# The last row block of a matmul with RMS norm: another split of the last product, squares shared between two engines, GpSimd for gamma, and the last stores reordered

## The chip, the cores and the metric

The kernel runs on one core of one Trainium2 chip. The core's engines work side by side: TensorE forms the matrix products, VectorE, ScalarE and GpSimd work element by element, SyncE issues transfers, and the DMA engines carry them out. A "store" is a transfer of finished output out of the core. The metric is device time of one execution in microseconds (us), as the median of several executions. Every ratio comes with a 95% interval. A "profile" is one execution recorded by the hardware profiler, which lists each instruction with its start, its length and what released it.

## The reference

```python
def reference(a, b, gamma, eps):          # a, b: 2048 x 2048 float32
    x = np.matmul(a, b)
    rms = np.sqrt(np.mean(x ** 2, axis=-1, keepdims=True) + eps)
    return (gamma * x / rms).astype(np.float32)
```

A row of the output can only be finished when its whole row of `x` is known, because `rms` needs the sum of all its squares.

## The kernel before

The product is cut into pairs of 128-row blocks, and each pair is formed with seven products in place of eight (sums and differences of quarter blocks). Columns are handled in four chunks of 512. The change touches only the end of the last pair: row block `rb`, whose four chunks can leave the core only after the very last product. That product completes chunk 3 (`x22[1]`). It is done in two halves, so that the first half is added and squared while TensorE works on the second.

The names in the excerpt are these. `p6` holds the result banks of the product. `t[1]` is what has to be added to it. `gam[c]` is gamma for chunk c. `xb` holds chunks 0 and 1, `x22[1]` chunk 3 and `p4[1]` chunk 2. `msq[rb]` holds the sums of squares of the chunks that are finished. `r_b` is the reciprocal of rms.

```python
        add(t[1], t[1], p4[1], ALU.subtract)            # VectorE
        square(rb, p4[1])                               # ScalarE: msq[rb][:, 2]
        pre_b = partial(rb)                             # VectorE: msq columns 0 and 1, and eps
        half_sq = stat_pool.tile([P, 2], FP32, name="n2")
        halves = [slice(0, CH // 2), slice(CH // 2, CH)]
        # [cut: TensorE, 8 matmuls for each half into p6]
        for h, col in enumerate(halves):
            add(x22[1][:, col], p6[h], t[1][:, col])    # VectorE
            sq = sq_pool.tile([P, 2 * CH], BF16, name="sq")   # a pool with ONE buffer
            nc.scalar.activation(out=sq[:, 0:CH // 2], in_=x22[1][:, col], func=ACTF.Square,
                                 scale=inv_sqrt_n, accum_out=half_sq[:, h:h + 1])
        part = stat_pool.tile([P, 1], FP32, name="part")
        nc.vector.tensor_scalar(out=part, in0=half_sq[:, 0:1], scalar1=pre_b,
                                scalar2=msq[rb][:, 2:3], op0=ALU.add, op1=ALU.add)
        add(x22[0], x22[0], gam[1], ALU.mult)           # VectorE: chunk 1 by gamma
        r_b = inverse_rms(half_sq[:, 1:2], part)        # ScalarE root, VectorE reciprocal
        x = xb[:, 0:CH]
        nc.vector.tensor_scalar_mul(out=x, in0=x, scalar1=r_b)
        nc.sync.dma_start(out=rows(rb, 0, CH), in_=x)   # store 1, SyncE's queue
        x = xb[:, CH:]
        by_r(x, r_b)                                    # ScalarE
        nc.scalar.dma_start(out=rows(rb, CH, HALF), in_=x)   # store 2, ScalarE's queue
        for c, x, src in ((3, x22[1], x22[1]), (2, x21[1], p4[1])):
            scaled_gamma(x, src, r_b, gam[c])           # VectorE: times r and gamma
            nc.sync.dma_start(out=rows(rb, c * CH, (c + 1) * CH), in_=x)   # stores 3, 4
```

The argument needs one thing that experiment 1 shows: where an instruction of an engine waits, those written behind it on that engine wait as well.

## Time and profile before

| What | Value |
|---|---|
| Time, median (range) of 3 runs | 224.39 us (224.30 to 224.49) |
| Span in the profile | 222.6 us |
| Share of the chain that ended last: TensorE | 83% |
| End of the last matmul (timeline) | 214.68 us |
| r usable | 216.35 us |
| Last four stores issued | 216.87, 217.11, 217.53, 218.19 us |
| Packets of these stores (DMA records) | 217.7 to 221.07 us |

This is the line of the profile page that gives the chain of work that ended last, by engine, for the kernel before. TensorE has 83% of it, and the change leaves TensorE's columns as they are, so only the tail after 214.68 us can move.

```profile
PE 83%; DMA 8%; DVE 2%; POOL 2%; issue 1%; ACT 1%; DVEq 0%; ACTq 0%; POOLq 0%
```

These lines are the timeline of the kernel before: start in us, length in us, engine (DVE is VectorE, ACT ScalarE, PE TensorE, SPq and ACTq the store queues of SyncE and ScalarE), source line, operation, output<-input, shapes, and in brackets the idle time ahead of it with what ended it.

```profile
214.02 0.60 ACT L291 ACTIVATE sq<-acc 128x512 bf16<-128x512 f32 x1 [0.67 <-DVE x L617]
214.03 0.42 DVE L617 TENSOR_TENSOR x<-acc,x 128x256 f32<-128x256 f32 x1
...
214.72 0.42 DVE L617 TENSOR_TENSOR x<-acc,x 128x256 f32<-128x256 f32 x1 [0.26 <-PE acc L677]
...
215.61 0.19 ACT L682 ACTIVATION_READ_ACCUMULATOR sq<-x 128x1 f32 x1
215.83 0.29 ACT L328 ACTIVATE rms<-n,part 128x1 f32<-128x1 f32 x1
216.16 0.16 DVE L322 RECIPROCAL r<-rms 128x1 f32<-128x1 f32 x1
...
216.35 0.48 DVE L690 TENSOR_SCALAR x<-x,r 128x512 f32<-128x512 f32 x1
...
216.87 0.33 SPq L691 DMA_DIRECT2D out_dram<-x  x1
217.11 0.36 ACTq L694 DMA_DIRECT2D out_dram<-x  x1
...
217.53 1.05 SPq L697 DMA_DIRECT2D out_dram<-x  x2
```

The first half is added at 214.03, before TensorE has finished. The second follows 0.04 us after the last matmul, at 214.72. ScalarE squares three things one after the other and has its last sum at 215.80. Then come root and reciprocal, and the first store leaves at 216.87. The last line merges two stores, 217.53 and 218.19.

The view by stretches of the kernel before has, for each us of the tail, the busy time of each engine with instruction counts, and in its last three columns the granted TensorE clock, the share of the DMA engines that is busy, and GB/s:

```profile
217.00:218.00 1.00, 0.00 (x0) 0.00 (x0) 1.00 (x2) 0.07 (x1) 0.00 (x0) 1.00 0.29 109
218.00:219.00 1.00, 0.00 (x0) 0.00 (x0) 0.16 (x1) 0.00 (x0) 0.00 (x0) 1.00 1.04 363
219.00:220.00 1.00, 0.00 (x0) 0.00 (x0) 0.00 (x0) 0.00 (x0) 0.00 (x0) 0.66 1.05 324
220.00:221.00 1.00, 0.00 (x0) 0.00 (x0) 0.00 (x0) 0.00 (x0) 0.00 (x0) 0.50 0.79 254
```

From 218 to 220 the DMA engines are full (the share can come out a little over 1), and after VectorE's last 0.16 us nothing else works: the 1.05 MB of the last row block are leaving the core.

### The profile page before, as it was taken

The page shows a single profiled execution, that of the slowest core. Times are in us where ns is not written, and L with a number is a line of the kernel's source. Part 1 is how long each engine was busy: PE and PEld are TensorE (multiplying, and loading weights), DVE is VectorE, ACT ScalarE, POOL GpSimd, SP SyncE. Part 2 cuts the span into 40 slices and gives each one's busy share as a digit, 9 for nine tenths or more (in the row PEclk, how much of TensorE's full clock was granted, in tenths as well). Part 3 has the DMA queues.
Part 4 walks back from the last instruction along what each step waited for, and adds up shares of the span by engine and source line. Part 5 has one row for each costly group of instructions (what it writes and reads, how often), then busy time and mean ns, then how long its engine had stood idle before and what let it go on. Part 6 is the DMA issues. An engine that isn't in the chain of part 4 may idle for free.

```text
span 222.6 us, 3026 instructions
## 1 busy us (share of the span) xinstructions
PE 211.1 (95%) x1043; PEld 98.6 (44%) x1043; DVE 161.8 (73%) x324; ACT 129.1 (58%) x272; POOL 24.5 (11%) x49
## 2 busy tenths in 40 slices
PE   7899999999999999999999999999999999999950
PEld 2445444444454444444444444444444444444430
DVE  2427557983999989978949298837994589587692
ACT  3110002807698895799646985699478954334570
POOL 7534232300000001000100002000200000000000
PEclk9999999999999999999999999999999999999997
DMA  6999999999973499818889259945994794044045
GB/s 184 223 202 209 203 208 211 212 303 259 327 280 159 188 272 292 310 72 226 276 228 400 58 174 222 366 151 143 246 368 168 97 282 189 0 188 193 0 190 188
DMA packets 36176, 47.13 MB, mean 212 GB/s; under 512 B 21952, under 2 KB 26048, under 8 KB 34496
## 3 DMA queue, kind: packets, MB, share of 16 engines
q0 software_dynamic: 9648, 23.33, 41.6%
q1 hardware_dynamic: 26080, 22.29, 33.0%
q10 hardware_dynamic: 432, 1.31, 2.0%
q8 instruction: 8, 0.13, 0.2%
q14 instruction: 8, 0.07, 0.1%
HBM read 34.60 MB, written 16.78 MB: 231 GB/s over the span
## 4 chain that ended last, share of the span: by engine, by line
PE 83%; DMA 8%; DVE 2%; POOL 2%; issue 1%; ACT 1%; DVEq 0%; ACTq 0%; POOLq 0%
PE acc L279 63%; PE acc L350 18%; DMA b<-in_b_dram 8%; POOL early L106 1%; DVE x L617 1%; POOL b L100 1%; DVE x L620 1%; PE tbank L179 1%; PE tbank L382 1%; PE tbank L165 1%; ACT sq L291 0%; DVEq L732 0%; ACT sq L682 0%; DVE x L690 0%; DVE r L322 0%
## 5 line engine op out<-in xcount | busy, mean ns | idle before, releaser
L279 PE MATMUL acc<-b,s 128*128 128x512 bf16 x376 | 83.3, 379 | 0.0
L279 PEld LDWEIGHTS <-s 128*128 128x128 f16 x472 | 46.2, 98 | 55.7 <-DVE s L244 0.2
L350 PE MATMUL acc<-b,head_at 128*128 128x512 bf16 x240 | 55.1, 379 | 0.6 <-DMA b<-in_b_dram 0.4
L291 ACT ACTIVATE sq<-x 128x512 bf16<-128x512 f32 x62 | 39.1, 631 | 10.9 <-DVE x L520 5.1
L340 DVE SCALAR_TENSOR_TENSOR x<-x,r,gamma_sb 128x1024 f32<-128x1024 f32 x28 | 34.7, 1282 | 0.8
L209 ACT ACTIVATE sq<-a 128x1024 bf16<-128x1024 f32 x24 | 25.4, 1057 | 16.8 <-DMA a<-in_a_dram 16.4
L350 PEld LDWEIGHTS <-head_at 128*128 128x128 bf16 x240 | 22.9, 98 | 26.7 <-issue 1.1
L393 ACT COPY x<-acc 128x512 f32<-128x512 f32 x11 | 5.9, 591 | 25.1 <-PE acc L350 25.1
L231 ACT ACTIVATE head_at<-a,s 128x2048 f16<-128x2048 f32 x10 | 19.9, 1990 | 0.0
L279 PEld LDWEIGHTS <-at_even 128*128 128x128 f16 x96 | 9.4, 98 | 11.5 <-issue 0.4
L279 PEld LDWEIGHTS <-head_at 128*128 128x128 f16 x96 | 9.4, 98 | 11.3
L100 POOL DMA_DIRECT2D b<-in_b_dram x15 | 10.6, 708 | 16.0 <-DMA b<-in_b_dram 13.2
L217 DVE TENSOR_SCALAR s<-norm 128x1 f32<-128x1 f32 x12 | 1.8, 150 | 14.3 <-ACT norm L212 14.2
L244 DVE TENSOR_TENSOR s<-at_even 128x1024 f16<-128x1024 f16 x15 | 9.7, 684 | 2.8 <-DMA at_even<-head_at 2.8
L291 ACT ACTIVATION_READ_ACCUMULATOR sq<-x 128x1 f32 x62 | 11.7, 188 | 0.0
L279 PE MATMUL acc<-t_left,s 128*128 128x512 bf16 x48 | 11.3, 379 | 0.0
L279 PE MATMUL acc<-early,s 128*128 128x512 bf16 x48 | 11.3, 379 | 0.0
L279 PE MATMUL acc<-early,at_even 128*128 128x512 bf16 x48 | 11.0, 379 | 0.0
L279 PE MATMUL acc<-t_left,at_even 128*128 128x512 bf16 x48 | 10.9, 379 | 0.0
L509 ACT COPY x<-acc 128x512 f32<-128x512 f32 x10 | 5.7, 575 | 8.9 <-PE acc L279 8.9
L279 PE MATMUL acc<-t_left,head_at 128*128 128x512 bf16 x48 | 10.8, 379 | 0.0
L279 PE MATMUL acc<-early,head_at 128*128 128x512 bf16 x48 | 10.8, 379 | 0.0
(86 smaller groups left out, 205.8 us busy)
## 6 DMA issues: line engine op xcount, KB each, us to landing
out_dram<-x SPq DMA_DIRECT2D x30, 512.0 KB, 3.1
a<-in_a_dram POOLq DMA_DIRECT2D x12, 1024.0 KB, 8.5
b<-in_b_dram POOLq DMA_DIRECT2D x15, 512.0 KB, 17.1
early<-in_a_dram POOLq DMA_DIRECT2D x7, 256.0 KB, 14.8
early<-in_b_dram ACTq DMA_DIRECT2D x2, 512.0 KB, 5.9
gamma_sb<-in_gamma_dram POOLq DMA_DIRECT2D x1, 1024.0 KB, 19.9
out_dram<-x SPq DMA_DIRECT2D x3, 256.0 KB, 3.5
early<-in_a_dram SPq DMA_DIRECT2D x1, 512.0 KB, 5.7
```

What stands on the lines that cost most here:

```text
L100: nc.gpsimd.dma_start(out=raw[j][kp], in_=b[kp * W2:(kp + 1) * W2, j * HALF:(j + 1) * HALF].rearrange("(t p) n -> p t n", p=P))
L106: nc.gpsimd.dma_start(out=ah(kp), in_=a[0:HB * P, kp * W2:(kp + 1) * W2].rearrange("(r p) k -> p r k", p=P))
L165: nc.tensor.matmul(view[:, t, r, :], ah(kp)[:, r, t * P:(t + 1) * P], identity, is_transpose=True, start=(t == 0 and r == 0), stop=(t == 1 ...
L209: nc.scalar.activation(out=junk, in_=a32[mb][:, h * HALF:(h + 1) * HALF], func=ACTF.Square, scale=2.0 ** -8, accum_out=n2[:, h:h + 1])
L231: nc.scalar.activation(out=a16[mb], in_=a32.pop(mb), func=ACTF.Copy, scale=factor.pop(mb))
L244: nc.vector.tensor_tensor(out=s_sum[s], in0=x, in1=y, op=op)
L279: nc.tensor.matmul(bank, lhsT[:, kp, :], rhs, start=(start and kp == 0), stop=(kp == KP - 1), skip_group_check=not start)
L291: nc.scalar.activation(out=sq[:, 0:CH], in_=src, func=ACTF.Square, scale=inv_sqrt_n, accum_out=msq[mb][:, c:c + 1])
L340: nc.vector.scalar_tensor_tensor(out=x, in0=x, scalar=r, in1=gamma_sb[:, h * HALF:(h + 1) * HALF], op0=ALU.mult, op1=ALU.mult)
L350: nc.tensor.matmul(bank, head_at[:, kt, r, :], head_rhs(c, kt), start=(kt == 0), stop=(kt == KT - 1))
L393: copy(out=x_chunk(*g), in_=banks[g])
L509: nc.scalar.copy(out=x21, in_=p2)
```

## The change

The intent can be read from the diff. VectorE should have less to do after r: GpSimd multiplies chunks 1 and 3 by gamma beforehand, and chunk 1 goes to ScalarE. The last sum of squares should come sooner: the product is cut into 320 and 192 columns, so the second piece is small, and VectorE squares it while ScalarE squares the first. And the last two stores should leave over both queues.

```diff
+        nc.gpsimd.tensor_tensor(out=x22[0], in0=x22[0], in1=gam[1], op=ALU.mult)
 ... [cut]
-        halves = [slice(0, CH // 2), slice(CH // 2, CH)]
-        for h, col in enumerate(halves):
-            add(x22[1][:, col], p6[h], t[1][:, col])
-            sq = sq_pool.tile([P, 2 * CH], BF16, name="sq")
-            nc.scalar.activation(... Square ..., accum_out=half_sq[:, h:h + 1])
-        part = stat_pool.tile([P, 1], FP32, name="part")
-        nc.vector.tensor_scalar(out=part, in0=half_sq[:, 0:1], scalar1=pre_b,
-                                scalar2=msq[rb][:, 2:3], op0=ALU.add, op1=ALU.add)
-        add(x22[0], x22[0], gam[1], ALU.mult)
-        r_b = inverse_rms(half_sq[:, 1:2], part)
+        x3 = a_pool.tile([P, K], FP32, name="a32")[:, 0:CH]
+        cut = 320
+        pieces = [slice(0, cut), slice(cut, CH)]
+        part = stat_pool.tile([P, 1], FP32, name="part")
+        nc.vector.tensor_scalar(out=part, in0=msq[rb][:, 2:3], scalar1=pre_b, scalar2=0.0,
+                                op0=ALU.add, op1=ALU.add)
+        for n, (bank, col) in enumerate(zip(p6, pieces)):
+            y = x22[1][:, col]
+            add(y, bank, t[1][:, col])
+            nc.gpsimd.tensor_tensor(out=x3[:, col], in0=y, in1=gam[3][:, col], op=ALU.mult)
+            sq = sq_pool.tile([P, 2 * CH], BF16, name="sq")
+            if n == 0:
+                nc.scalar.activation(out=sq[:, col], in_=y, func=ACTF.Square,
+                                     scale=inv_sqrt_n, accum_out=sums_b[:, 0:1])
+            else:
+                nc.vector.tensor_tensor_reduce(
+                    out=sq[:, col], in0=y, in1=y, scale=1.0 / float(N), scalar=part,
+                    op0=ALU.mult, op1=ALU.add, accum_out=sums_b[:, 1:2])
+        r_b = inverse_rms(sums_b[:, 1:2], sums_b[:, 0:1])
 ... [cut: the four stores of before]
+        nc.vector.tensor_scalar_mul(out=x3, in0=x3, scalar1=r_b)
+        nc.sync.dma_start(out=rows(rb, 3 * CH, N), in_=x3)
+        by_r(xb[:, 0:CH], r_b)
+        nc.sync.dma_start(out=rows(rb, 0, CH), in_=xb[:, 0:CH])
+        scaled_gamma(x21[1], p4[1], r_b, gam[2])
+        nc.sync.dma_start(out=rows(rb, 2 * CH, 3 * CH), in_=x21[1])
+        by_r(xb[:, CH:], r_b)
+        nc.scalar.dma_start(out=rows(rb, CH, HALF), in_=xb[:, CH:])
```

More of the change, by code (lines that the diff above doesn't have):

```diff
@@ L670, in last_group @@
         pre_b = partial(rb)
-        half_sq = stat_pool.tile([P, 2], FP32, name="n2")
-        halves = [slice(0, CH // 2), slice(CH // 2, CH)]
-        p6 = [new_bank()[:, 0:CH // 2] for _ in halves]
-        for bank, col in zip(p6, halves):
+        x3 = a_pool.tile([P, K], FP32, name="a32")[:, 0:CH]
+        sums_b = stat_pool.tile([P, 2], FP32, name="n2")
+        cut = 320
+        pieces = [slice(0, cut), slice(cut, CH)]
+        p6 = [new_bank()[:, 0:col.stop - col.start] for col in pieces]
+        for bank, col in zip(p6, pieces):
             for kp in range(KP):
@@ L678, in last_group @@
                                  start=(kp == 0), stop=(kp == KP - 1))
-        for h, col in enumerate(halves):
-            add(x22[1][:, col], p6[h], t[1][:, col])
-            sq = sq_pool.tile([P, 2 * CH], BF16, name="sq")
-            nc.scalar.activation(out=sq[:, 0:CH // 2], in_=x22[1][:, col], func=ACTF.Square,
-                                 scale=inv_sqrt_n, accum_out=half_sq[:, h:h + 1])
-        part = stat_pool.tile([P, 1], FP32, name="part")
-        nc.vector.tensor_scalar(out=part, in0=half_sq[:, 0:1], scalar1=pre_b,
-                                scalar2=msq[rb][:, 2:3], op0=ALU.add, op1=ALU.add)
@@ L687, in last_group @@
-        add(x22[0], x22[0], gam[1], ALU.mult)
-        r_b = inverse_rms(half_sq[:, 1:2], part)
-        x = xb[:, 0:CH]
-        nc.vector.tensor_scalar_mul(out=x, in0=x, scalar1=r_b)
-        nc.sync.dma_start(out=rows(rb, 0, CH), in_=x)
-        x = xb[:, CH:]
-        by_r(x, r_b)
-        nc.scalar.dma_start(out=rows(rb, CH, HALF), in_=x)
-        for c, x, src in ((3, x22[1], x22[1]), (2, x21[1], p4[1])):
-            scaled_gamma(x, src, r_b, gam[c])
-            nc.sync.dma_start(out=rows(rb, c * CH, (c + 1) * CH), in_=x)
+        part = stat_pool.tile([P, 1], FP32, name="part")
```

## The prediction

> **What bounds it.** The change only touches the last 10 us; the page's chain of waits puts 83% of the span on TensorE, whose last product is the same 4,096 columns after the change (16 matmuls, 212.77 to 214.68 in the timeline). So only the tail from 214.68 to 222.6 can move. In the timeline of before, that tail is: second half's add 214.72, its square and accumulator read on ScalarE to 215.80, root 215.83, reciprocal 216.16, r usable at 216.35. Then four 256 KB stores are issued at 216.87, 217.11, 217.53 and 218.19. The DMA records show packets without a break from 217.7 to 221.06: 1.05 MB, 3.4 us. So the end is set about equally by the first issue (through DMA throughput) and by the last one (218.19). After the last packet 1.55 us follow that no change here touches.
>
> **What the change does.** After r, VectorE has one 0.74 us operation fewer (now 0.48 + 0.74), ScalarE one 0.72 us operation more. GpSimd takes two multiplies by gamma. The last issue should then come about 0.9 us after the first, not 1.3 us.
>
> **What it costs before r.** I read two new waits in the order of the built instructions:
> 1. The sum "part" now stands on VectorE ahead of both adds, and it needs the square of the product before the last (p4), whose accumulator read ends on ScalarE at 214.71. Before, the first add ran at 214.03. Now the 320-column add starts only at about 214.93 (0.49 us, between the measured 0.42 for 256 and 0.68 for 512) and the 192-column one at about 215.34.
> 2. The VectorE square-sum waits for ScalarE's square of the 320, because both write the same scratch buffer. ScalarE: 215.46 to 216.01. So the two squares run in series, not in parallel.
>
> Then square-sum of 192 about 0.42 us with its accumulator read (estimate from the 0.42 us of a 256-column operation), root 0.3, reciprocal 0.16: r usable at about 217.03, 0.7 us later than before. First store at about 217.55 (before 216.87), last at about 218.4 on ScalarE's queue (before 218.19).
>
> **GpSimd.** The Trainium skill, "GPSIMD Engine Reference", Elementwise — side-by-side cycle accounting, has 4,497 ns for 2,048 fp32 columns of a two-input operation; my estimate is 1.15 us for 512, 0.75 for 320, 0.5 for 192. The first hides (213.4 to 214.6). The others end at about 216.7, just before r. No GpSimd multiply is in the trace of before, so this is not tested. The skill, "SBUF — State Buffer", Terms, says VectorE and GpSimd take their shared port pair exclusively; the square-sum has two on-chip-buffer inputs and meets those multiplies, which may hold it up by 0.1 to 0.6 us.
>
> **Sum.** r 0.7 us later, last issue 0.2 us later, stores packed more tightly (2.8 to 3.4 us): the end moves by 0.1 to 0.7 us, with contention perhaps 1 us. Predicted 224.8 us, range 224.35 to 225.5. Chances: faster by over 2% 0.01, within 2% 0.98, slower by over 2% 0.01.
>
> **What would show it.** Timeline: "part" waiting for ScalarE's accumulator read and ending after 214.9; 320-column add near 214.93; VectorE's square-sum starting only after ScalarE's 320 read; r near 217.0; first store near 217.55; all issues within 0.9 us; packets unbroken from 218.3 to 221.2-221.7.
>
> **What would make it wrong.** Faster than before if stores at the end cost by last issue alone, or go at over 370 GB/s on two queues. Slower than 225.5 if GpSimd's multiplies last twice my estimate or block VectorE throughout, delaying r or the first store.

## The result

The changed kernel takes 224.91 us (224.86 to 225.08, 4 runs) against 224.41 us for before on the same chip (224.30 to 224.49, 4 runs). The ratio is 1.0025, with a 95% interval of 1.001 to 1.0039. (The ratio is the one from the runs of both kernels in the same rounds of measurement; it is not quite the ratio of the medians.) The change therefore costs about half a microsecond. The profiled run of the changed kernel was its slowest, 225.08 us, so the difference of the two profiles (222.6 to 223.3) somewhat overstates the 0.5 us between the medians.

The chain line of the page for the changed kernel has the same shares at its head, as it should:

```profile
PE 83%; DMA 8%; POOL 2%; DVE 2%; ACT 1%; issue 1%; ACTq 0%; POOLq 0%
```

The timeline of the changed kernel, from the same place on (POOL is GpSimd, CUSTOM_DVE_ANT_0 is VectorE's square-sum):

```profile
213.48 1.27 POOL L665 TENSOR_TENSOR x<-x,gamma_sb 128x512 f32<-128x512 f32 x1 [53.39 <-ACT sq L291]
...
214.51 0.19 ACT L291 ACTIVATION_READ_ACCUMULATOR sq<-acc 128x1 f32 x1
214.74 0.21 DVE L683 TENSOR_SCALAR part<-msq,part 128x1 f32<-128x1 f32 x1 [0.63 <-ACT sq L291]
214.87 0.74 DVE L617 TENSOR_TENSOR x<-acc,x 128x320 f32<-128x320 f32 x2
215.43 1.52 POOL L688 TENSOR_TENSOR a<-x,gamma_sb 128x320 f32<-128x320 f32 x2 [0.68 <-DVE x L617]
215.45 0.47 ACT L691 ACTIVATE sq<-x 128x320 bf16<-128x320 f32 x1 [0.74 <-DVE x L617]
215.82 0.19 ACT L691 ACTIVATION_READ_ACCUMULATOR sq<-x 128x1 f32 x1
216.04 0.47 DVE L694 CUSTOM_DVE_ANT_0 sq<-x,part 128x192 bf16<-128x192 f32 x1 [0.42 <-ACT sq L691]
216.44 0.08 DVE L694 DVE_READ_ACCUMULATOR2_ANT n<- 128x1 f32 x1
...
216.88 0.16 DVE L322 RECIPROCAL r<-rms 128x1 f32<-128x1 f32 x1 [0.36 <-ACT rms L328]
...
217.16 0.49 DVE L698 TENSOR_SCALAR a<-a,r 128x512 f32<-128x512 f32 x1
...
217.67 0.33 SPq L699 DMA_DIRECT2D out_dram<-a  x1
218.10 0.38 SPq L701 DMA_DIRECT2D out_dram<-x  x1
218.44 0.39 ACTq L705 DMA_DIRECT2D out_dram<-x  x1
218.57 0.40 SPq L703 DMA_DIRECT2D out_dram<-x  x1
```

Two brackets on VectorE carry the story. Line L683 (the sum `part`) sat idle 0.63 us for ScalarE's square of `p4`, and the add behind it, which in the kernel before had started at 214.03, starts at 214.87. Line L694 (the square-sum) sat idle 0.42 us for ScalarE's square of the 320 columns. The reciprocal starts at 216.88 instead of 216.16, and the first store leaves at 217.67 instead of 216.87. The stores then follow each other within 0.90 us instead of 1.32.

The same view by stretches, changed kernel:

```profile
218.00:219.00 1.00, 0.00 (x0) 0.00 (x0) 0.30 (x1) 0.41 (x1) 0.00 (x0) 0.81 0.49 184
219.00:220.00 1.00, 0.00 (x0) 0.00 (x0) 0.00 (x0) 0.00 (x0) 0.00 (x0) 0.50 1.07 371
220.00:221.00 1.00, 0.00 (x0) 0.00 (x0) 0.00 (x0) 0.00 (x0) 0.00 (x0) 0.50 1.05 320
221.00:222.00 1.00, 0.00 (x0) 0.00 (x0) 0.00 (x0) 0.00 (x0) 0.00 (x0) 0.50 0.47 174
```

The pattern is that of before, moved by about 0.75 us. DMA records give packets from 218.50 to 221.80, which is 3.3 us; before had 3.4.

### The profile page after: what moved, and what is told of

Same layout as the page of the kernel before. It is cut to its first block, busy times and chain, and to the rows that moved or that the text cites. A ratio compares the mean times of both kernels' runs of the same rounds, so it can differ in the third digit from the quotient of the medians. Undisturbed runs are those within 1.5% of the kernel's fastest.

```text
span 223.3 us, 3033 instructions
## 1 busy us (share of the span) xinstructions
PE 212.3 (95%) x1043; PEld 98.9 (44%) x1043; DVE 160.8 (72%) x324; ACT 129.2 (58%) x271; POOL 27.3 (12%) x52
## 4 chain that ended last, share of the span: by engine, by line
PE 83%; DMA 8%; POOL 2%; DVE 2%; ACT 1%; issue 1%; ACTq 0%; POOLq 0%
PE acc L279 63%; PE acc L350 18%; DMA b<-in_b_dram 8%; POOL early L106 1%; DVE x L617 1%; POOL b L100 1%; PE tbank L179 1%; PE tbank L382 1%; PE tbank L165 1%; DVE x L620 1%; ACT sq L291 0%; ACT x L624 0%; ACT rms L328 0%; ACT sq L691 0%; DVE sq L694 0%
## 5 line engine op out<-in xcount | busy, mean ns | idle before, releaser
L393 ACT COPY x<-acc 128x512 f32<-128x512 f32 x11 | 5.9, 591 | 25.0 <-PE acc L350 25.0
L121 POOL COPY pace<-x 128x1 f32<-128x1 f32 x4 | 0.7, 183 | 88.5 <-DVE x L525 88.5
```

Source lines behind the costliest of these rows:

```text
L393: copy(out=x_chunk(*g), in_=banks[g])
```

## The experiments

Chips and executions differ by a few tenths of a us ahead of the tail: the last matmul ended between 214.47 and 215.31 in the profiles, in kernels that are the same up to there. So profiles are compared by times counted from the end of the last matmul. That end is modelled by the profiler, in the same way in each. The table is worked out from the timelines and DMA records. "r done" is the end of the reciprocal. "Ratio" is the time against the kernel before in the same rounds.

```
us after the last matmul's end   r     first  last   first   last    first issue to  ratio (95%)
                                done   issue  issue  packet  packet  last packet
before                          1.64   2.19   3.51   3.01    6.39    4.20            1
changed kernel                  2.36   2.99   3.89   3.82    7.12    4.13            1.0025 (1.0010-1.0039)
part_after_adds                 1.64   2.27   3.17   3.10    6.42    4.15            1.0007 (0.9995-1.0019)
own_scratch                     2.41   3.04   3.94   3.87    7.19    4.15            1.0041 (1.0027-1.0054)
no_gpsimd_chunk3                2.31   3.12   4.02   3.95    7.34    4.22            1.0047 (1.0034-1.0061)
own_scratch_no_gpsimd           1.99   2.80   3.70   3.63    7.01    4.21            1.0030 (1.0018-1.0042)
early_sum                       1.72   2.34   3.24   3.16    6.51    4.17            1.0006 (0.9992-1.0020)
half_stores (wrong output)      2.35   2.98   3.88   3.81    5.59    2.61            0.9971 (0.9958-0.9984)
three_stores                    1.65   2.28   2.94   3.10    6.01    3.73            0.9984 (0.9972-0.9996)
three_stores_again              1.65   2.27   2.93   3.10    6.02    3.75            0.9983 (0.9971-0.9995)
early_sum_three                 1.70   2.32   2.99   3.15    6.03    3.71            0.9986 (0.9972-1.0000)
after_three_stores              2.36   2.99   3.65   3.81    6.71    3.72            1.0015 (0.9998-1.0031)
before_three_stores             1.63   2.45   3.11   3.28    6.25    3.80            1.0008 (0.9993-1.0023)
```

### 1. The sum `part` behind the adds (part_after_adds)

```diff
-        nc.vector.tensor_scalar(out=part, in0=msq[rb][:, 2:3], scalar1=pre_b, ...)
         for n, (bank, col) in enumerate(zip(p6, pieces)):
             add(y, bank, t[1][:, col])
             ...
             else:
+                nc.vector.tensor_scalar(out=part, in0=msq[rb][:, 2:3], scalar1=pre_b, ...)
                 nc.vector.tensor_tensor_reduce(...)
```

> The changed kernel with one instruction moved: VectorE's sum 'part' (which waits for ScalarE's square of p4) stands behind the two adds instead of ahead of them. My theory: the in-order wait of VectorE is most of the loss. The 320-column add starts at about 214.03 instead of 214.87, the 192-column add at 214.72, ScalarE's square of 320 ends at about 215.31, the square-sum runs 215.34 to 215.81, r is usable at about 216.35 (0.7 us earlier), first store about 216.95. Time about 224.2 to 224.4, so 0.5 to 0.7 us below the changed kernel and level with before. Rival (the stores' new order or GpSimd's multiplies cost the 0.5 us): r moves, but the time stays near 224.9.

Measured: 224.38 us against 224.28, ratio 1.0007. From the timeline of this kernel:

```profile
214.15 0.49 DVE L617 TENSOR_TENSOR x<-acc,x 128x320 f32<-128x320 f32 x1
...
214.81 1.52 POOL L686 TENSOR_TENSOR a<-x,gamma_sb 128x320 f32<-128x320 f32 x2
214.81 0.36 DVE L617 TENSOR_TENSOR x<-acc,x 128x192 f32<-128x192 f32 x1 [0.17 <-PE acc L680]
...
215.44 0.44 DVE L694 CUSTOM_DVE_ANT_0 sq<-x,part 128x192 bf16<-128x192 f32 x1 [0.15 <-ACT sq L689]
...
216.25 0.16 DVE L322 RECIPROCAL r<-rms 128x1 f32<-128x1 f32 x1 [0.36 <-ACT rms L328]
...
217.04 0.33 SPq L699 DMA_DIRECT2D out_dram<-a  x1
```

The second add now waits for TensorE alone, and r is ready 1.64 us after the last matmul: 0.72 us sooner than in the changed kernel, and exactly as in before. The position of one tiny instruction is all that r lost, and the last packet of the stores comes 6.42 us after the last matmul, against 7.12 in the changed kernel and 6.39 in before. (The intervals of the two ratios, 1.0025 and 1.0007, overlap; the profiles are what separates them.) It also shows that the rest of the change gains nothing yet: with r as early as before, this kernel is level with before, not faster.

### 2. One scratch tile for both squares (own_scratch)

```diff
+        sq = sq_pool.tile([P, 2 * CH], BF16, name="sq")
         for n, (bank, col) in enumerate(zip(p6, pieces)):
             ...
-            sq = sq_pool.tile([P, 2 * CH], BF16, name="sq")
```

> The changed kernel with one scratch tile allocated for both squares (they write disjoint columns), so that VectorE's square-sum no longer waits for ScalarE's square of 320; 'part' stays ahead of the adds. Theory: the square-sum starts at about 215.66 instead of 216.04 and r comes 0.35 us earlier, at about 216.7; time about 224.55. Rival (GpSimd's multiply of 320, 215.43 to 216.29, blocks a VectorE operation with two inputs in the on-chip buffer): the square-sum starts at 215.66 but ends no earlier than 216.3, and r and the time hardly move.

Measured: 225.02 us, ratio 1.0041. The theory missed and its rival was right. From the timeline:

```profile
215.22 1.52 POOL L689 TENSOR_TENSOR a<-x,gamma_sb 128x320 f32<-128x320 f32 x2 [0.68 <-DVE x L617]
...
215.44 0.85 DVE L694 CUSTOM_DVE_ANT_0 sq<-x,part 128x192 bf16<-128x192 f32 x1
...
216.72 0.16 DVE L322 RECIPROCAL r<-rms 128x1 f32<-128x1 f32 x1 [0.42 <-ACT rms L328]
```

The wait is gone, and the square-sum starts as early as expected. But it now takes 0.85 us instead of 0.47, and r is ready 2.41 us after the last matmul (2.36 in the changed kernel). GpSimd's multiply of the 320 columns, 215.22 to 216.08, lies over it.

### 3. The same without GpSimd's multiplies of chunk 3 (own_scratch_no_gpsimd)

```diff
 (own_scratch)
-            nc.gpsimd.tensor_tensor(out=x3[:, col], in0=y, in1=gam[3][:, col], op=ALU.mult)
-        nc.vector.tensor_scalar_mul(out=x3, in0=x3, scalar1=r_b)
+        x3 = x22[1]
+        scaled_gamma(x3, x3, r_b, gam[3])
```

> The kernel with one scratch for both squares (own_scratch), with GpSimd's two multiplies of chunk 3 taken away as well (VectorE applies r and gamma in one operation after r). There VectorE's square-sum took 0.85 us instead of 0.47. If that was GpSimd holding the shared path (theory), it now takes 0.42 us, and from the start of the sum 'part' to the start of the reciprocal it is 1.70 to 1.75 us instead of 2.19. Rival (the square-sum is slow because ScalarE reads the same tile at that moment): it stays at 0.8 us. Time: r 0.4 us earlier than own_scratch, the end of VectorE 0.3 us later after r, so about 224.7 to 224.9.

Measured: 225.00 us, ratio 1.0030. The time is a little above the range I gave. The mechanism is as expected:

```profile
215.71 0.42 DVE L692 CUSTOM_DVE_ANT_0 sq<-x,part 128x192 bf16<-128x192 f32 x1
...
216.56 0.16 DVE L322 RECIPROCAL r<-rms 128x1 f32<-128x1 f32 x1 [0.42 <-ACT rms L328]
```

The square-sum takes 0.42 us, although ScalarE reads the same tile then, as it did in own_scratch. So the 0.43 us extra there came from GpSimd. The other traces say the same. In all nine kernels in which GpSimd multiplies chunk 3, the square-sum ends 0.21 to 0.22 us after the recorded end of GpSimd's 320-column multiply, although it starts anywhere from 0.22 to 0.64 us before that end. With its 0.42 us it would in each case have been through sooner, by 0.02 us in part_after_adds, 0.05 in the changed kernel and 0.43 in own_scratch. So that multiply sets the end of the square-sum in all of them, and only what it costs differs. This also settles what two of the changed kernel's parts do to each other: the VectorE square-sum can run beside ScalarE's square, or GpSimd can multiply at that moment, but the two do not go together. That r is 0.42 us earlier than in own_scratch brings the first store only 0.24 us forward (3.04 to 2.80), because VectorE's fused operation after r takes 0.75 us where the prepared one took 0.48.

### 4. The changed kernel without GpSimd's multiplies of chunk 3 (no_gpsimd_chunk3)

The edit is that of experiment 3, applied to the changed kernel.

> The changed kernel without GpSimd's two multiplies of chunk 3; VectorE applies r and gamma to chunk 3 in one operation after r, as before the change. Theory (GpSimd costs next to nothing): adds and square-sum keep their durations within 0.05 us, r within 0.05 us of 217.05; first store about 217.85 instead of 217.67, last about 218.55; time 224.8 to 225.1, so within 0.2 us. Rival (sharing with GpSimd is what makes VectorE and r late): r comes 0.3 us or more earlier and the time falls to 224.5 or less.

Measured: 225.20 us, 0.1 us above the range I gave for my theory and far from the rival's; ratio 1.0047 against 1.0025 for the changed kernel in other rounds. In the changed kernel itself GpSimd costs r only 0.05 us (2.36 against 2.31; the square-sum took 0.47 us against 0.42), because the square-sum was waiting for ScalarE anyway while GpSimd was at work. In return GpSimd makes the first store 0.13 us earlier (2.99 against 3.12). So sharing with GpSimd is not why the changed kernel is late.

### 5. Half of the bytes in the last four stores (half_stores)

```diff
-        nc.sync.dma_start(out=rows(rb, 3 * CH, N), in_=x3)
+        nc.sync.dma_start(out=rows(rb, 3 * CH, 3 * CH + CH // 2), in_=x3[:, 0:CH // 2])
 ... [the other three in the same way]
```

> Wrong on purpose: the changed kernel, but each of the last four stores writes only the first 256 of its 512 columns; issue times are unchanged. If the end is set by how fast the stores' 1.05 MB move from the first issue on (theory), half the bytes end the packets 1.2 to 1.7 us earlier, time about 223.3 to 223.7. If the end is set by the last issue and a fixed landing time (rival), the time falls by under 0.5 us, to about 224.5.

Measured: 223.66 us, ratio 0.9971, and outputs that are wrong. The time is in the range of the throughput theory, 1.2 us below the changed kernel (0.0054 of the time, by the two ratios), where its rival allowed under 0.5 us. The issues are where they were; the packets take 1.78 us instead of 3.29. By stretches, this kernel:

```profile
219.00:220.00 1.00, 0.00 (x0) 0.00 (x0) 0.00 (x0) 0.00 (x0) 0.00 (x0) 0.50 0.93 308
220.00:221.00 1.00, 0.00 (x0) 0.00 (x0) 0.00 (x0) 0.00 (x0) 0.00 (x0) 0.50 0.56 184
```

So the end follows from when the first store leaves and how long the bytes take. The table says the same: in every kernel with four full stores, the last packet comes 4.13 to 4.22 us after the first issue, whether the last issue follows the first by 0.90 us (the changed kernel and its variants) or by 1.32 us (before). No run changes this spacing alone, though: the kernels with 0.90 us also send the stores in another order over the two queues.

### 6. Three stores (three_stores, three_stores_again)

```diff
 (part_after_adds)
-        by_r(xb[:, 0:CH], r_b)
-        nc.sync.dma_start(out=rows(rb, 0, CH), in_=xb[:, 0:CH])
         scaled_gamma(x21[1], p4[1], r_b, gam[2])
         nc.sync.dma_start(out=rows(rb, 2 * CH, 3 * CH), in_=x21[1])
-        by_r(xb[:, CH:], r_b)
-        nc.scalar.dma_start(out=rows(rb, CH, HALF), in_=xb[:, CH:])
+        by_r(xb, r_b)
+        nc.scalar.dma_start(out=rows(rb, 0, HALF), in_=xb)
```

> The part_after_adds kernel, with chunks 0 and 1 scaled by one ScalarE operation and stored as one 512 KB store on ScalarE's queue; chunks 3 and 2 as before on the other queue. If part of the end's 3.4 us of packets is lost to turning from one store to the next (rates of about 200 GB/s between 219.5 and 220.0), this takes 0.1 to 0.4 us off: packets for about 3.0 us, time about 224.0 to 224.2 where part_after_adds had 224.38. Rival (only bytes and the first issue matter, the dips come whatever the stores are): within 0.1 us of part_after_adds.

Measured: 223.98 us against 224.31, ratio 0.9984 (0.9972 to 0.9996). The stores in the timeline, and the stretches of this kernel:

```profile
216.84 0.33 SPq L699 DMA_DIRECT2D out_dram<-a  x1
217.49 0.38 ACTq L703 DMA_DIRECT2D out_dram<-x  x1
217.50 0.33 SPq L701 DMA_DIRECT2D out_dram<-x  x1
```

```profile
217.00:218.00 1.00, 0.00 (x0) 0.00 (x0) 0.47 (x1) 0.46 (x1) 0.00 (x0) 1.00 0.32 121
218.00:219.00 1.00, 0.00 (x0) 0.00 (x0) 0.00 (x0) 0.00 (x0) 0.00 (x0) 1.00 1.10 387
219.00:220.00 1.00, 0.00 (x0) 0.00 (x0) 0.00 (x0) 0.00 (x0) 0.00 (x0) 0.71 1.00 397
220.00:221.00 1.00, 0.00 (x0) 0.00 (x0) 0.00 (x0) 0.00 (x0) 0.00 (x0) 0.50 0.37 143
```

In the second full microsecond the rate holds at 397 GB/s, where before has 324. The same bytes take 2.90 us instead of 3.32 in part_after_adds: 1.05 MB over these is 361 against 315 GB/s.

> The three_stores kernel once more, beside the other two on one chip. It gave 0.9984 (0.9972 to 0.9996); a second interval below 1 would confirm it as the first version faster than the kernel before, by about 0.3 us.

Measured: 224.06 us against 224.46, ratio 0.9983 (0.9971 to 0.9995). Both intervals lie below 1. This is the best version, about 0.35 us (0.16%) below the kernel before, so "the same" at the level of 2%. The dip that the expectation names is in the trace of part_after_adds, though shorter: 225 and 184 GB/s in the two tenths of a us from 219.5 on. Several things differ at once: the number of stores, the length of a row in the merged store (4 KB instead of 2 KB), the shares of the two queues (512 KB on each instead of 768 and 256), and the last issue, 0.66 us after the first instead of 0.90. Which of them counts was not separated.

### 7. Both waits off and no `part` on VectorE (early_sum)

`spare` is a piece of a tile that is free by then.

```diff
 (own_scratch, with:)
-        x3 = a_pool.tile([P, K], FP32, name="a32")[:, 0:CH]
+        x3 = spare
-        nc.vector.tensor_scalar(out=part, in0=msq[rb][:, 2:3], scalar1=pre_b, ...)
             if n == 0:
                 nc.scalar.activation(... Square ..., accum_out=sums_b[:, 0:1])
+                nc.scalar.activation(out=sum_0, in_=sums_b[:, 0:1], func=ACTF.Identity,
+                                     bias=msq[rb][:, 2:3], scale=1.0)
-            ... scalar=part,
+            ... scalar=pre_b,
-        r_b = inverse_rms(sums_b[:, 1:2], sums_b[:, 0:1])
+        r_b = inverse_rms(sums_b[:, 1:2], sum_0)
```

> Both waits taken off and no 'part' on VectorE at all: the square-sum starts from the sum of the earlier squares, ScalarE adds the square of p4 to its own sum while it is idle, both squares write one scratch tile, and the product with gamma lies in a tile without waits on old loads. Square-sum starts at 215.1 to 215.25 on the clock of the profile before (limited by GpSimd's first multiply), ends by about 215.65, r usable at about 216.2 (before 216.35), first store at about 216.7. Theory (the end follows the first issue): time 0.15 to 0.3 us below part_after_adds, about 224.1. If GpSimd's multiply holds the square-sum to its end, r is as in part_after_adds and the time about 224.3.

Measured: 224.39 us, ratio 1.0006, as part_after_adds. From the timeline of this kernel, whose last matmul ends at 214.52:

```profile
213.33 1.28 POOL L665 TENSOR_TENSOR x<-x,gamma_sb 128x512 f32<-128x512 f32 x1 [53.41 <-ACT sq L291]
...
214.56 1.52 POOL L687 TENSOR_TENSOR head_at<-x,gamma_sb 128x320 f32<-128x320 f32 x2
...
215.06 0.57 DVE L694 CUSTOM_DVE_ANT_0 sq<-x,part 128x192 bf16<-128x192 f32 x1 [0.15 <-DVE x L617]
```

The rival had it: the square-sum started 0.54 us after the last matmul, 0.12 us earlier than in part_after_adds, but took 0.57 us instead of 0.44 beside GpSimd's multiply, and the root then waited for two engines. r is ready at 1.72 us instead of 1.64. The add that GpSimd's 320-column multiply needs had ended 0.13 us before the end of the last matmul, but the multiply begins only as GpSimd's own multiply of chunk 1 ends, 0.05 to 0.09 us after it. The square-sum then ends 0.21 us after the recorded end of the 320-column multiply, at 1.12 us (part_after_adds: 1.11), although it started earlier. The split of the squares over two engines therefore gave no earlier r in any of its forms that keep GpSimd's multiplies: before, with all squares on ScalarE, has 1.64 as well. No run has the early sum without those multiplies, so what the split alone is worth stays open.

### 8. early_sum with three stores (early_sum_three)

> early_sum with the three stores of three_stores. If both effects are real they add: about 223.8 to 224.1, the first version below the kernel before. If either is nil, as the better of the two.

Measured: 224.08 us, ratio 0.9986 (0.9972 to 1.0). As the better of the two alone, which is what was to be expected once early_sum by itself gave nothing.

### 9. The changed kernel with three stores (after_three_stores)

> The changed kernel as it is, with only the last stores changed to three (chunks 0 and 1 in one 512 KB store on ScalarE's queue). If the late r (0.7 us) and the stores' packets (3.3 against 2.9 us) are two separate terms, this is about 0.4 us below the changed kernel: ratio to before about 1.0005, and the last packet about 6.7 us after the last matmul (7.12 in the changed kernel). If merging helps only when r is early, it stays at 1.0025.

Measured: 224.74 us against 224.46, ratio 1.0015 (0.9998 to 1.0031). In the profile the last packet comes 6.71 us after the last matmul, 0.41 less than in the changed kernel, as expected of two separate terms. The ratio of the times moved in that direction by less (0.0010), and the two intervals overlap, so the times alone do not show it.

### 10. The kernel before with three stores (before_three_stores)

```diff
 (before)
-        x = xb[:, 0:CH]
-        nc.vector.tensor_scalar_mul(out=x, in0=x, scalar1=r_b)
-        nc.sync.dma_start(out=rows(rb, 0, CH), in_=x)
-        x = xb[:, CH:]
-        by_r(x, r_b)
-        nc.scalar.dma_start(out=rows(rb, CH, HALF), in_=x)
+        by_r(xb, r_b)
+        nc.scalar.dma_start(out=rows(rb, 0, HALF), in_=xb)
```

> The kernel before with only its chunks 0 and 1 merged into one ScalarE operation and one 512 KB store. VectorE then starts with chunk 3's 0.74 us operation with gamma, so the first store comes 0.2 us later than in before (0.8 us after r). If packets take 2.9 us instead of 3.4, the last packet comes about 6.15 us after the last matmul (before 6.39) and the ratio is about 0.999. If the merged store alone makes the best version, it equals three_stores (0.998); if GpSimd's multiplies are worth something there, it stays 0.1 to 0.2 us behind three_stores.

Measured: 224.62 us against 224.46, ratio 1.0008 (0.9993 to 1.0023). A miss: I expected 0.999. The packets take 2.97 us, as expected, but the first store comes 0.26 us later than in before, since VectorE's first operation after r is now the 0.75 us one. That eats most of the gain: the last packet comes at 6.25 us instead of 6.39. The end of the span then follows the last data packet by 1.77 us, where the kernels here mostly have 1.49 to 1.58; why is open. It suggests, and with that end left open does not show, that the merged store pays only together with a short first operation after r. In three_stores that is the 0.49 us multiply by r, which GpSimd's multiply of chunk 3 makes possible; this would make that part of the change worth having, once r is no longer late.

## Why the prediction was right or wrong, point by point

The time, 224.91 us, lay in the range (224.35 to 225.5) and 0.1 us from the predicted 224.8. The direction and the mechanism of the late r were right; the reading of the end was wrong, and other steps were off in size. That the number came within 0.1 us is partly luck: 0.4 us was a middle between a first issue 0.7 us later and a last issue 0.2 us later, and of these only the first counted. In the profiles the last packet came 0.73 us later. The times differ by 0.5 us, with an interval of 0.2 to 0.9 us (from the ratio's) that holds both figures.

- **Wait 1, `part` ahead of the adds: right.** Predicted: the 320-column add at 214.93, the 192-column one at 215.34. Measured: 214.87 and 215.27. Moving the instruction gave back all 0.72 us of r.
- **Wait 2, the shared scratch buffer: there, but worth nothing alone.** Predicted: ScalarE's square from 215.46 to 216.01, square-sum after it. Measured: 215.45 to 216.01, square-sum at 216.04. The prediction counted the serial squares as a cost of their own. Without the wait, r came no earlier (2.41 against 2.36 us), since GpSimd stood in its place.
- **r usable at 217.03: right**, ScalarE used it at 217.08. The first store was 0.12 us later than predicted (217.67 against 217.55). VectorE's first operation started at 217.16, 0.12 us after the reciprocal had ended. This operation also waits for old loads of the buffer that `x3` was put in, and for GpSimd. The loads are little of it: in early_sum, where the buffer has no such waits, the gap is still 0.11 us. In all four kernels with no GpSimd multiply of chunk 3 (before, no_gpsimd_chunk3, own_scratch_no_gpsimd, before_three_stores) it is 0.035. So the gap goes with the wait for GpSimd, although GpSimd had ended at 216.95; why is open.
- **"the end is set about equally by the first issue ... and by the last one": wrong.** This is the step that failed. The last packet came 4.13 to 4.22 us after the first issue in all kernels with four full stores, whatever the last issue did. The 0.42 us by which the change narrows the issues (1.32 to 0.90 us) came with at most 0.07 us less from first issue to last packet (4.20 to 4.13; 4.15 to 4.22 in the variants). The term that counts is the packets' 3.3 us, which halved bytes and merged stores did move.
- **GpSimd's durations: mis-sized.** Estimated 1.15, 0.75 and 0.5 us for 512, 320 and 192 columns; measured 1.27, 0.86 and 0.70. They ended at 216.95, not 216.7, still 0.1 us before r was ready.
- **"which may hold it up by 0.1 to 0.6 us": mis-sized for this kernel.** It was 0.05 us here (0.47 against 0.42), because ScalarE's wait had already held the square-sum for most of the multiply. In own_scratch, where it meets the multiply earlier, it is 0.43 us.
- **The last issue: right time, wrong queue.** ScalarE's store was at 218.44 (predicted 218.4), but the last was SyncE's third, at 218.57: its three stores leave 0.43 and 0.47 us apart. The data of the third had been ready since 218.30, and it left 0.09 us after the issue ahead of it on that queue had ended (218.48).

The sum, with what was measured in the two profiles: first store 0.80 us later, last packet 0.73 us later, span 0.7 us longer, medians 0.5 us apart.

## What to carry to other kernels

An instruction that waits for another engine belongs behind the ones that don't need it: the 0.2 us sum put ahead of two adds cost 0.7 us. Before work is shared out to a third engine, look at what will run beside it, because a wait that is taken away can give way to another one that stood hidden behind it, as in own_scratch. At an end that is bound by stores, count from the first issue and the bytes: an earlier first store and fewer, larger stores shortened this tail, and bringing the last issue closer to the first, as the change did, made no difference that the profiles show beyond 0.07 us.

## What the Trainium skill lacked or had wrong

- "SBUF — State Buffer", Terms and Who interferes with whom, says that a VectorE instruction with two inputs in the on-chip buffer and a GpSimd instruction that reads it take a shared port in turn, the loser being blocked for the whole instruction. A block is there: 0.85 us instead of 0.42 in own_scratch. But in all nine kernels in which GpSimd multiplies chunk 3 (experiment 3) the square-sum ended 0.21 to 0.22 us after GpSimd's recorded end, and it needs 0.42 us by itself, so about half of it ran while GpSimd's instruction was still recorded as busy. GpSimd's recorded spans are rough, so this is what a recorded span tells of the block; it doesn't show the page's lock to be otherwise than it says. The page has no such figure.
- "GPSIMD Engine Reference", Elementwise — side-by-side cycle accounting, has 4,497 ns for 2,048 fp32 columns as the one length of a two-input operation. Scaled down by columns, that gives an estimate of 1.12, 0.70 and 0.42 us for 512, 320 and 192 columns; recorded were 1.27, 0.86 and 0.70. The fewer the columns, the longer each takes (2.5, 2.7 and 3.7 ns). The page names a dispatch step of each GpSimd instruction, but has no figure for it.
- "DMA: Bandwidth & Descriptors", Rules for kernel authors, advises to coalesce many small transfers and warns of overhead under 64 KB. The runs agree, at larger sizes than it warns of: four 256 KB stores moved at 309 to 318 GB/s (1.05 MB over the packets' time), two of 256 KB and one of 512 KB at 353 to 364. What of the merging brings this was not separated (experiment 6). The page has no figure for several stores in a row.
- No page has the length of VectorE's multiply-and-sum with its accumulator read: 0.42 us for 192 fp32 columns with no GpSimd multiply beside it, the read being recorded from 0.35 to 0.43 us after its start.
